# Seven block products of a SwiGLU FFN on one core: another order, three PSUM banks instead of four, and transposes placed later

## The chip, the cores and the metric

One core of a Trainium2 chip runs the whole program. The metric is device microseconds for one execution. A profiled execution gives a trace beside its time; its span, from the program's first to its last instruction, is a little shorter than its time. The engines are TensorE (PE: matmuls and transposes; PEld: its weight loads), VectorE (DVE), ScalarE (ACT), GpSimd (POOL) and SyncE (SP), whose queue issues most DMAs.

## The reference

Two layers, each made of a SwiGLU FFN at half weight, a token mixer, and another such FFN, with a layer norm after each. There are 256 tokens (two tiles of 128, t = 0 and 1) of width 1024; the FFN's inner width is 2816. So there are four FFNs in all:

```python
def swiglu(x, wg, wu, wd):
    return (jax.nn.silu(x @ wg) * (x @ wu)) @ wd
...
x = layer_norm(ALPHA * x + 0.5 * swiglu(x, ffn_wg[l, 0], ffn_wu[l, 0], ffn_wd[l, 0]), ln_g[l, 0], ln_b[l, 0])
```

Everything is float32.

## The kernel before, in words

**Precision.** A float32 product is done as three matmuls: each operand is split in a high and a low part (`xh`, `xl`; `wh`, `wl`), and high times high, high times low and low times high are summed in PSUM (`mm3`, L263). For weights the split is one ACT copy that rounds (`wh`) and one DVE subtraction (`wl`), on tiles of 128x1024 (`split_tile` L217, `split_half` L223). Weights come by DMA into `raw` tiles, of which there are three; `wh` and `wl` have eight buffers each.

**Units.** A unit is 1 MB of weights (two tiles). `units` holds how each one is loaded and split, in the order of use. Using unit u emits the splits up to u + 4 in the middle of an FFN (`ahead` is 3). The inner width is cut in eleven chunks of 256 (gate and up columns side by side: 512 PSUM columns). `down(c)` is the unit that multiplies chunk c's gated values into the output.

**The FFN.** `glu(t, c, q)` adds half q of the input width to chunk c's 512 columns for token tile t: 12 matmuls. After q = 1 the gate follows: silu on ACT (`sg`), and one DVE operation that multiplies (`hh`). `h_T(t, g)` transposes the gated values of chunk pair g on PE and splits them into `hi` (ACT) and `lo` (DVE); `down(t, c)` reads these. A down costs 24 matmuls for both token tiles.

**Strassen's stage.** For chunks 4 and 5, and again for 8 and 9, `strassen` replaces the 8 block products (two token tiles, two halves of the width, two chunks) by seven, after Winograd. The left operands are sums of blocks of x, made once per FFN by `make_sums` (L312); the right ones are sums of weight blocks, made on DVE by `less` (L141) in the functions f1 to f7 of `seven` (L132) and split by `parts`. The seven are spread among four downs of earlier chunks by `SEVEN` (L41): None is a product, a number a down.

**Order.** In the middle of the FFN (`middle` L511) PE's instructions keep the program's order. The order on ACT, DVE and SP is set ahead of time by a scheduler, which goes by program order, by `high_priority`, and by its own estimate of when operands and buffers are ready; on the chip each queue then runs in that fixed order. Groups of chunks follow `GROUPS` (L39): normal chunks 2 and 3, stage 4/5, normal 6 and 7, stage 8/9, normal 10, then the last downs (`end` L534), which are not pinned.

**PSUM.** Eight banks: four hold the output sums (`acc`), four (`g` and `tr`, for t = 0 and 1) are handed out in the order of a list, `self.free` (L376); who is done with a bank appends it.

The places that the change touches: `SEVEN`, `seven`, `strassen` (L421), `gated` (L473), the place of `h_T` and `make_sums` in `middle`, and the scratch size in `kernel`.

Of the kernel before, what the change touches and what calls it, by code (L numbers as in the profile page):

```python
# [18 lines left out]
F32 = mybir.dt.float32  # L19
# [3 lines left out]
AF = mybir.ActivationFunctionType  # L23
ALU = mybir.AluOpType
# [30 lines left out]
def build(ctx, tc, d):  # L55
    nc = tc.nc
    PE, ACT, DVE, POOL = nc.tensor, nc.scalar, nc.vector, nc.gpsimd

    cst = ctx.enter_context(tc.tile_pool(name="cst", bufs=1))
    wp = ctx.enter_context(tc.tile_pool(name="wp", bufs=1))  # L60
    act = ctx.enter_context(tc.tile_pool(name="act", bufs=1))
    mix = ctx.enter_context(tc.tile_pool(name="mix", bufs=2))
# [61 lines left out]
    units = []  # L124
# [4 lines left out]
    def gate_up(l, f, c, q):  # L129
        return [d["wgu"][l, f, c, 2 * q + h] for h in range(2)]  # L130

    def seven(l, f, c):  # L132

        A, B, C, E = [], [], [], []

        def load(to, src, pool, **kw):
            for a in src:
                to.append(pool.tile([128, 1024], F32, **kw))
                last_dma[0] = nc.sync.dma_start(out=to[-1], in_=a)

        def less(a, b, to):  # L141
            for x, y, z in zip(a, b, to):
                DVE.tensor_sub(out=z, in0=x, in1=y)  # L143

        def parts(ts):
            return [split_tile(x, 1024) for x in ts]

        def f1():
            for h, a in enumerate(gate_up(l, f, c, 0)):
                load(A, [a], mix, name="fa", tag=f"qs{h}", bufs=1)  # L150
            return parts(A)

        def f2():
            load(B, gate_up(l, f, c + 1, 0), wp, name="raw", bufs=3)
            less(B, A, A)
            return parts(A)

        def f3():
            load(C, gate_up(l, f, c + 1, 1), mix, name="fc", tag="pT", bufs=3)
            less(C, B, B)  # L160
            return parts(B)

        def f4():
            less(C, A, A)
            return parts(A)

        def f5():
            load(E, gate_up(l, f, c, 1), wp, name="raw", bufs=3)
            return parts(E)

        def f6():
            return parts(C)

        def f7():
            less(E, A, A)
            return parts(A)
        return f1, f2, f3, f4, f5, f6, f7

    for l in range(L):
        def ffn_units(f):  # L180
            def down(c):
                if c >= 0:
                    halves([d["wd"][l, f, (2 * c + h) * 128:(2 * c + h + 1) * 128, :] for h in range(2)], 1024)
            for kind, *cs in GROUPS:
                if kind == "s":
                    fs = iter(seven(l, f, cs[0]))
                    for x in SEVEN:
                        if x is None:
                            units.append(next(fs))
                        else:  # L190
                            down(cs[0] - 4 + x)
# [178 lines left out]
    class Ffn:  # L370
# [50 lines left out]
        def strassen(self, c):  # L421

            s1, s2, s3, s4 = self.s
            a = [[tuple(p[:, 4 * q:4 * q + 4] for p in XT[t]) for q in range(2)] for t in range(2)]
            tags = iter(("c40", "c41", "at011", "vblk"))
            downs = iter(range(c - 4, c))

            def f32(name):
                return mix.tile([128, 512], F32, name=name, tag=next(tags), bufs=1)

            def down():
                n = next(downs)
                self.down(0, n)
                self.down(1, n)
            (w1, b1), (w5, b5) = self.bank(), self.bank()
            self.product(b1, a[0][0])
            with tc.high_priority():
                c11 = f32("c11")
                ACT.activation(out=c11, in_=b1, func=AF.Copy)
            for t in range(2):  # L440
                self.h_T(t, c // 2 - 1)
            down()
            self.product(b5, s1)
            down()
            w7, b7 = self.bank()
            self.product(b7, s3)
            self.product(b1, s2, False)
            with tc.high_priority():
                u = f32("u")
                ACT.activation(out=u, in_=b1, func=AF.Copy)  # L450
                c22 = f32("c22")
                DVE.tensor_add(out=c22, in0=b5, in1=u)
                DVE.tensor_add(out=c22, in0=b7, in1=c22)
            self.gated(1, c + 1, c22)
            down()
            w2, b2 = self.bank()
            self.product(b2, a[0][1])
            with tc.high_priority():
                DVE.tensor_add(out=c11, in0=b2, in1=c11)
            self.gated(0, c, c11)  # L460
            self.product(b5, s4, False)
            with tc.high_priority():
                c12 = f32("c12")
                DVE.tensor_add(out=c12, in0=b5, in1=u)
            self.gated(0, c + 1, c12)
            down()
            self.product(b7, a[1][1], False)
            with tc.high_priority():
                DVE.tensor_add(out=u, in0=b7, in1=u)
            self.gated(1, c, u)  # L470
            self.free.extend((w1, w2, w5, w7))

        def gated(self, t, c, x):  # L473
            with tc.high_priority():
                ACT.activation(out=x[:, 0:256], in_=x[:, 0:256], func=AF.Silu)
                DVE.scalar_tensor_tensor(out=x[:, 0:256], in0=x[:, 0:256], scalar=0.5, in1=x[:, 256:512], op0=ALU.mult,
                                         op1=ALU.mult)
            self.hh.setdefault((t, c // 2), [None, None])[c % 2] = x

        def h_T(self, t, g):  # L480
            src = self.hh.pop((t, g))
# [27 lines left out]
                    c == 0 and kk == 0, c == NCH - 1 and kk == 1)  # L509

        def middle(self):  # L511
            self.s = make_sums(self.sums)
            ahead[0] = 3
            pinned[0] = True
            for kind, *cs in GROUPS[1:]:
                if kind == "s":
                    self.strassen(cs[0])
                    continue
                for c in cs:
                    for q in range(2):  # L520
                        for t in range(2):
                            self.glu(t, c, q)
                        if c % 2 == 0 and q == 0:
                            for t in range(2):
                                self.h_T(t, c // 2 - 1)
# [495 lines left out]
    for l in range(L):  # L1021
# [3 lines left out]
        out = [wout(m, t) for t in range(2)]  # L1025
# [104 lines left out]
```

## Time and profile before

| | before |
|---|---|
| median of 3 runs | 994.06 us (993.55 to 994.34) |
| profiled execution | 994.04 us |
| its span | 991.9 us |
| mean granted clock of PE | 0.997 |
| PE, DVE, ACT, POOL busy | 98%, 79%, 55%, 4% |
| HBM read | 176.91 MB |

Busy is the share of the span in which the engine has an instruction under way. A matmul of 512 columns is shown with some 0.39 us, but the next one starts before it ends; the distance between starts tells what one costs. In a timeline a bracket at the end of a row gives the idle time of the engine ahead of it, and what ended it.

### The profile page before, as it was taken

The page shows a single profiled execution, that of the slowest core. Times are in us where ns is not written, and L with a number is a line of the kernel's source. Part 1 is how long each engine was busy: PE and PEld are TensorE (multiplying, and loading weights), DVE is VectorE, ACT ScalarE, POOL GpSimd, SP SyncE. Part 2 cuts the span into 40 slices and gives each one's busy share as a digit, 9 for nine tenths or more (in the row PEclk, how much of TensorE's full clock was granted, in tenths as well). Part 3 has the DMA queues.
Part 4 walks back from the last instruction along what each step waited for, and adds up shares of the span by engine and source line. Part 5 has one row for each costly group of instructions (what it writes and reads, how often), then busy time and mean ns, then how long its engine had stood idle before and what let it go on. Part 6 is the DMA issues. An engine that isn't in the chain of part 4 may idle for free.

```text
span 991.9 us, 12822 instructions
## 1 busy us (share of the span) xinstructions
PE 971.4 (98%) x4659; PEld 789.1 (80%) x4659; DVE 784.3 (79%) x1195; ACT 549.0 (55%) x840; POOL 34.8 (4%) x50
## 2 busy tenths in 40 slices
PE   8999999999999999999999999999999999999996
PEld 5888878878778888878888788888787788788885
DVE  6698867897869879688797877868888687788775
ACT  6555455475755655565555654644667355555550
POOL 0000000020002000000000000001000010000000
PEclk9999999999999999999999999999999999999999
DMA  8757657554445727537574572675535365473551
GB/s 293 244 163 252 174 171 245 167 191 154 147 152 157 227 84 273 188 138 275 160 223 148 174 253 83 194 237 161 195 102 160 126 222 158 136 251 127 190 171 43
DMA packets 51871, 178.79 MB, mean 180 GB/s; under 512 B 6624, under 2 KB 7648, under 8 KB 51552
## 3 DMA queue, kind: packets, MB, share of 16 engines
q1 hardware_dynamic: 49968, 171.23, 53.1%
q0 software_dynamic: 1840, 6.75, 2.2%
q8 instruction: 36, 0.59, 0.2%
q14 instruction: 27, 0.22, 0.1%
HBM read 176.91 MB, written 1.05 MB: 179 GB/s over the span
## 4 chain that ended last, share of the span: by engine, by line
PE 30%; DVE 10%; DMA 7%; ACT 2%; issue 2%; DVEq 0%; ACTq 0%; SPq 0%
PE acc L266 5%; PE acc L264 5%; PE acc L265 5%; DMA raw<-in_wgu 5%; DVE wl L232 3%; PE tr L418 3%; PE g L418 2%; DMA raw<-in_wd 2%; PE g L265 1%; DVE fa L143 1%; DVE wl L220 1%; PE g L266 1%; PE g L264 1%; ACT wh L231 1%; PE tr L292 1%
## 5 line engine op out<-in xcount | busy, mean ns | idle before, releaser
L232 DVE TENSOR_TENSOR wl<-raw,wh 128x1024 fp32r<-128x1024 f32 (+2 forms) x257 | 308.3, 1206 | 113.0 <-ACT wh L231 112.3
L231 ACT ACTIVATE wh<-raw 128x1024 fp32r<-128x1024 f32 (+2 forms) x257 | 267.9, 1045 | 223.0 <-DMA raw<-in_wgu 76.0
L264 PE MATMUL acc<-wh,hi 128*128 128x512 f32 x352 | 139.4, 396 | 0.0
L265 PE MATMUL acc<-wl,hi 128*128 128x512 f32 x352 | 138.1, 392 | 0.8 <-DVE wl L232 0.8
L266 PE MATMUL acc<-wh,lo 128*128 128x512 f32 x352 | 138.5, 393 | 0.1
L265 PE MATMUL g<-wl,xh 128*128 128x512 f32 (+1 forms) x320 | 122.9, 384 | 1.7 <-DVE wl L232 1.7
L264 PE MATMUL g<-wh,xh 128*128 128x512 f32 (+1 forms) x320 | 123.7, 387 | 0.0
L266 PE MATMUL g<-wh,xl 128*128 128x512 f32 (+1 forms) x320 | 122.5, 383 | 0.0
L219 ACT ACTIVATE wh<-fa 128x1024 fp32r<-128x1024 f32 x64 | 65.2, 1051 | 45.8 <-DVE fa L143 16.9
L220 DVE TENSOR_TENSOR wl<-fa,wh 128x1024 fp32r<-128x1024 f32 x64 | 76.4, 1219 | 4.6 <-ACT wh L219 4.3
L266 PEld LDWEIGHTS acc<-wh,lo 128*128 128x128 f32 x352 | 66.5, 189 | 15.2 <-DVE lo L270 1.2
L265 PEld LDWEIGHTS acc<-wl,hi 128*128 128x128 f32 x352 | 66.4, 189 | 14.6 <-DVE wl L232 1.1
L264 PEld LDWEIGHTS acc<-wh,hi 128*128 128x128 f32 x352 | 66.5, 189 | 13.9 <-ACT wh L231 0.4
L265 PEld LDWEIGHTS g<-wl,xh 128*128 128x128 f32 x320 | 60.3, 188 | 13.7 <-DVE wl L232 3.1
L264 PEld LDWEIGHTS g<-wh,xh 128*128 128x128 f32 x320 | 60.1, 188 | 11.7 <-issue 0.8
L266 PEld LDWEIGHTS g<-wh,xl 128*128 128x128 f32 x320 | 60.1, 188 | 10.8
L264 PE MATMUL tr<-wh,xh 128*128 128x512 f32 x160 | 63.3, 396 | 0.0
L266 PE MATMUL tr<-wh,xl 128*128 128x512 f32 x160 | 62.4, 390 | 0.0
L265 PE MATMUL tr<-wl,xh 128*128 128x512 f32 x160 | 62.3, 390 | 0.0
L143 DVE TENSOR_TENSOR fa<-raw,fa 128x1024 f32<-128x1024 f32 x32 | 38.6, 1221 | 18.8 <-DMA raw<-in_wgu 18.8
L265 PE MATMUL acc<-wl,xh 128*128 128x512 f32 x128 | 51.3, 401 | 1.2 <-DVE wl L232 1.2
L264 PE MATMUL acc<-wh,xh 128*128 128x512 f32 x128 | 50.7, 398 | 0.4 <-ACT wh L231 0.4
(293 smaller groups left out, 1683.4 us busy)
## 6 DMA issues: line engine op xcount, KB each, us to landing
raw<-in_wgu SPq DMA_DIRECT2D x143, 512.0 KB, 4.2
raw<-in_wd SPq DMA_DIRECT2D x88, 512.0 KB, 4.1
raw<-in_win SPq DMA_DIRECT2D x32, 512.0 KB, 3.9
fa<-in_wgu SPq DMA_DIRECT2D x16, 512.0 KB, 4.3
fc<-in_wgu SPq DMA_DIRECT2D x16, 512.0 KB, 4.7
raw<-in_wout SPq DMA_DIRECT2D x16, 512.0 KB, 4.4
lnp_ln_g<-in_ln_g POOLq DMA_DIRECT2D x5, 512.0 KB, 5.4
lnp_ln_b<-in_ln_b POOLq DMA_DIRECT2D x5, 512.0 KB, 5.8
```

The source lines that it names most:

```text
L143: DVE.tensor_sub(out=z, in0=x, in1=y)
L219: ACT.activation(out=wh[:, :w], in_=raw[:, :w], func=AF.Copy)
L220: DVE.tensor_sub(out=wl[:, :w], in0=raw[:, :w], in1=wh[:, :w].bitcast(F32))
L231: ACT.activation(out=wh[:, s], in_=raw[:, s], func=AF.Copy)
L232: DVE.tensor_sub(out=wl[:, s], in0=raw[:, s], in1=wh[:, s].bitcast(F32))
L264: pe(PE.matmul(ps, xh, wh, start=start, stop=False))
L265: pe(PE.matmul(ps, xh, wl, start=False, stop=False))
L266: pe(PE.matmul(ps, xl, wh, start=False, stop=stop))
L292: last_pe[0] = PE.transpose(p[:, i * 128:(i + 1) * 128], s, ident)
L418: pe(PE.matmul(ps, a[:, k, :], w[:, s], start=first and k == 0 and n == 0, stop=k == 3 and n == 2, skip_group_check=True))
```

## The change

- In the stage of seven products bank b1 sums products 1, 6, 7 and 4, with copies of its state by ACT after 1, 6 and 7; b5 sums 5 and 3; b2 holds 2. Before, b1 summed two, b5 two, a fourth bank b7 two, and b2 held one. Three DVE adds are left of five, three ACT copies instead of two. Product 4's gate reads its bank directly.
- The order of products and downs is 1 5 d 6 d 7 d 2 3 d 4; before it was 1 d 5 d 7 6 d 2 3 d 4 in the same names.
- The second weight block (`b12`) gets buffers of its own, `fb0` and `fb1`, instead of two of the three `raw`. The scratch for software DMAs is set to 8192.
- `h_T` of the previous chunk pair comes after product 5 instead of 1 in the stage, and in normal groups after t = 0's second half instead of after both first halves.
- `make_sums` comes after chunk 2 instead of ahead of it.

```diff
-SEVEN = (None, 0, None, 1, None, None, 2, None, None, 3, None)
+SEVEN = "1 5 d 6 d 7 d 2 3 d 4".split()
...
+        def f5():
+            load(b12, gate_up(l, f, c + 1, 0), wp, "fb", ("fb0", "fb1"), 1)
+            less(b12, b11, b11)
+            return parts(b11)
+
+        def f6():
+            load(b22, gate_up(l, f, c + 1, 1), mix, "fc", ("pT", "pT"), 3)
+            less(b22, b11, b11)
+            return parts(b11)
+
+        def f7():
+            less(b22, b12, b12)
+            return parts(b12)
 
         def f2():
-            load(B, gate_up(l, f, c + 1, 0), wp, name="raw", bufs=3)
-            less(B, A, A)
-            return parts(A)
...
+            load(b21, gate_up(l, f, c, 1), wp, "raw", ("raw", "raw"), 3)
+            r = parts(b21)
+            less(b21, b11, b11)
+            return r
...
+        return {"1": f1, "5": f5, "6": f6, "7": f7, "2": f2, "3": lambda: parts(b22), "4": lambda: parts(b11)}
...
+            left = {"1": a[0][0], "5": s1, "6": s2, "7": s3, "2": a[0][1], "3": s4, "4": a[1][1]}
...
+            def copy(b):
+
+                r = f32()
+                ACT.activation(out=r, in_=b, func=AF.Copy)
+                return r
+
             (w1, b1), (w5, b5) = self.bank(), self.bank()
...
+            for x in SEVEN:
+                if x == "d":
+                    self.down(0, n)
+                    self.down(1, n)
+                    n += 1
+                    continue
+                if x == "2":
+                    w2, b2 = self.bank()
+                self.product({"5": b5, "3": b5, "2": b2 if x == "2" else None}.get(x, b1), left[x], x in "152")
+                with tc.high_priority():
+                    if x == "1":
+                        c11 = copy(b1)
+                    elif x == "6":
+                        u = copy(b1)
+                    elif x == "7":
+                        c22 = copy(b1)
+                        DVE.tensor_add(out=c22, in0=b5, in1=c22)
+                        self.gated(1, c + 1, c22)
+                    elif x == "2":
+                        DVE.tensor_add(out=c11, in0=b2, in1=c11)
+                        self.gated(0, c, c11)
+                        self.free.append(w2)
+                    elif x == "3":
+                        DVE.tensor_add(out=u, in0=b5, in1=u)
+                        self.gated(0, c + 1, u)
+                        self.free.append(w5)
+                    elif x == "4":
+                        self.gated(1, c, b1, f32())
+                        self.free.append(w1)
+                if x == "5":
+                    for t in range(2):
+                        self.h_T(t, c // 2 - 1)
...
         def middle(self):
-            self.s = make_sums(self.sums)
...
                     for q in range(2):
                         for t in range(2):
                             self.glu(t, c, q)
-                        if c % 2 == 0 and q == 0:
-                            for t in range(2):
-                                self.h_T(t, c // 2 - 1)
+                            if c % 2 == 0 and (q, t) == (1, 0):
+                                self.h_T(0, c // 2 - 1)
+                                self.h_T(1, c // 2 - 1)
+                    if c == 2:
+                        self.s = make_sums(self.sums)
...
-    nc = bacc.Bacc("TRN2", target_bir_lowering=False, num_devices=1)
+    nc = bacc.Bacc("TRN2", target_bir_lowering=False, num_devices=1, dynamic_dma_scratch_size=8192)
```

## Rows read from the trace of the kernel before

**Rows 1.** The page, part 1: busy time, share of the span, instructions.

```profile
PE 971.4 (98%) x4659; PEld 789.1 (80%) x4659; DVE 784.3 (79%) x1195; ACT 549.0 (55%) x840; POOL 34.8 (4%) x50
```

**Rows 2.** Busy time by stretch: length, each engine (count), clock, DMA share, GB/s.

```profile
542.80:588.50 45.70, 43.84 (x190) 35.73 (x189) 38.12 (x39) 26.79 (x31) 0.00 (x0) 0.96 0.59 196
...
611.10:653.20 42.10, 42.10 (x190) 34.64 (x189) 32.76 (x35) 24.16 (x28) 0.53 (x1) 1.00 0.58 197
```

**Rows 3.** Timeline of PE around 547: start, us, line, operation, [idle before].

```profile
545.49 0.60 PE L487 MATMUL g<-ident,hh 128*128 128x128 f32 x4
547.95 0.66 PE L487 MATMUL g<-ident,hh 128*128 128x128 f32 x4 [1.86 <-DVE hh L404]
```

**Rows 4.** Busy time by stretch, just behind those transposes.

```profile
548.60:552.00 3.40, 3.40 (x10) 2.63 (x9) 1.76 (x4) 1.82 (x3) 0.00 (x0) 0.50 0.39 151
```

**Rows 5.** List of waits: waiter, releaser: us in total, times, longest us.

```profile
PE g L487 <- DVE hh L404: 4.6, 4, 1.9
```

**Rows 6.** Timeline of DVE at the same place.

```profile
545.21 1.22 DVE L143 TENSOR_TENSOR fa<-fc,fa 128x1024 f32<-128x1024 f32 x1
546.35 1.22 DVE L232 TENSOR_TENSOR wl<-raw,wh 128x1024 fp32r<-128x1024 f32 x1
547.48 0.41 DVE L404 SCALAR_TENSOR_TENSOR hh<-sg,g 128x256 f32<-128x256 f32 x1
```

**Rows 7.** Timelines of SP, ACT and PE from 120 to 136.

```profile
120.92 16.10 SPq L228 DMA_DIRECT2D raw<-in_wd  x4
...
133.21 1.06 ACT L231 ACTIVATE wh<-raw 128x1024 fp32r<-128x1024 f32 x1 [4.49 <-DMA raw<-in_wd]
...
133.92 0.39 PE L266 MATMUL acc<-wh,lo 128*128 128x512 f32 x1
...
135.58 0.50 PE L265 MATMUL acc<-wl,hi 128*128 128x512 f32 x1 [0.76 <-DVE wl L232]
```

**Rows 8.** Timelines of PE and DVE around chunk 2's gate, third FFN.

```profile
528.94 0.39 PE L266 MATMUL tr<-wh,xl 128*128 128x512 f32 x1
...
533.38 1.22 DVE L143 TENSOR_TENSOR fa<-raw,fa 128x1024 f32<-128x1024 f32 x1 [2.37 <-DMA raw<-in_wgu]
534.52 0.41 DVE L404 SCALAR_TENSOR_TENSOR hh<-sg,tr 128x256 f32<-128x256 f32 x1
```

**Rows 9.** Timelines of PE, ACT and DVE around chunk 10, third FFN.

```profile
658.62 0.60 PE L487 MATMUL g<-ident,c 128*128 128x128 f32 x4
659.06 0.38 PE L487 MATMUL tr<-ident,u 128*128 128x128 f32 x2
...
659.41 0.48 PE L264 MATMUL tr<-wh,xh 128*128 128x512 f32 x1
...
659.96 0.39 PE L266 MATMUL tr<-wh,xl 128*128 128x512 f32 x1
...
662.23 0.39 PE L264 MATMUL g<-wh,xh 128*128 128x512 f32 x1
...
665.63 0.50 PE L266 MATMUL acc<-wh,lo 128*128 128x512 f32 x1
...
662.66 1.06 ACT L231 ACTIVATE wh<-raw 128x1024 fp32r<-128x1024 f32 x1 [1.81 <-DMA raw<-in_wd]
663.62 0.58 ACT L269 ACTIVATE hi<-g 128x512 fp32r<-128x512 f32 x1
...
664.89 0.68 DVE L270 TENSOR_TENSOR lo<-g,hi 128x512 fp32r<-128x512 f32 x1
```

**Rows 10.** Busy time by stretch in the first FFN, columns as in rows 2.

```profile
12.00:34.00 22.00, 20.36 (x87) 16.13 (x88) 16.19 (x20) 12.15 (x18) 0.00 (x0) 1.00 0.87 300
34.00:56.10 22.10, 22.10 (x103) 18.36 (x102) 17.51 (x18) 13.02 (x17) 0.00 (x0) 1.00 0.71 225
```

**Rows 11.** Groups of instructions: line, operation, shapes, count | busy us, mean ns.

```profile
L459 DVE TENSOR_TENSOR c<-g,c 128x512 f32<-128x512 f32 x8 | 5.5, 683 | 0.0
L439 ACT ACTIVATE c<-tr 128x512 f32<-128x512 f32 x8 | 4.8, 598 | 14.8 <-PE tr L418 14.8
```

More of the change, by code (lines that the diff above doesn't have):

```diff
@@ L132, in seven, with load @@
     def seven(l, f, c):
[L134 to L138, printed above, removed]
+        b11, b12, b21, b22 = [], [], [], []
+        def load(to, src, pool, name, tags, bufs):
+            for a, tag in zip(src, tags):
+                to.append(pool.tile([128, 1024], F32, name=name, tag=tag, bufs=bufs))
                 last_dma[0] = nc.sync.dma_start(out=to[-1], in_=a)
@@ L148, in f1 @@
         def f1():
-            for h, a in enumerate(gate_up(l, f, c, 0)):
-                load(A, [a], mix, name="fa", tag=f"qs{h}", bufs=1)
-            return parts(A)
-        def f2():
-            load(B, gate_up(l, f, c + 1, 0), wp, name="raw", bufs=3)
-            less(B, A, A)
[L156 to L177, printed above, removed]
+            load(b11, gate_up(l, f, c, 0), mix, "fa", ("qs0", "qs1"), 1)
+            return parts(b11)
[6 more added lines that the diff above has]
+            less(b22, b11, b11)
+            return parts(b11)
+        def f7():
+            less(b22, b12, b12)
+            return parts(b12)
+        def f2():
+            load(b21, gate_up(l, f, c, 1), wp, "raw", ("raw", "raw"), 3)
[3 more added lines that the diff above has]
+        return {"1": f1, "5": f5, "6": f6, "7": f7, "2": f2, "3": lambda: parts(b22), "4": lambda: parts(b11)}
     for l in range(L):
@@ L185, in ffn_units @@
                 if kind == "s":
-                    fs = iter(seven(l, f, cs[0]))
+                    fs = seven(l, f, cs[0])
+                    n = cs[0] - 4
                     for x in SEVEN:
-                        if x is None:
-                            units.append(next(fs))
+                        if x == "d":
+                            down(n)
+                            n += 1
                         else:
-                            down(cs[0] - 4 + x)
+                            units.append(fs[x])
                 else:
@@ L424, in strassen @@
             a = [[tuple(p[:, 4 * q:4 * q + 4] for p in XT[t]) for q in range(2)] for t in range(2)]
+            left = {"1": a[0][0], "5": s1, "6": s2, "7": s3, "2": a[0][1], "3": s4, "4": a[1][1]}
             tags = iter(("c40", "c41", "at011", "vblk"))
[L426 to L434, printed above, removed]
@@ L435, in strassen @@
-            (w1, b1), (w5, b5) = self.bank(), self.bank()
[L436 to L439, printed above, removed]
-            for t in range(2):
-                self.h_T(t, c // 2 - 1)
[L442 to L478, printed above, removed]
+            def f32():
+                return mix.tile([128, 512], F32, name="cc", tag=next(tags), bufs=1)
@@ new lines, in copy @@
+            def copy(b):
+                r = f32()
+                ACT.activation(out=r, in_=b, func=AF.Copy)
+                return r
+            (w1, b1), (w5, b5) = self.bank(), self.bank()
+            n = c - 4
+            for x in SEVEN:
+                if x == "d":
+                    self.down(0, n)
+                    self.down(1, n)
+                    n += 1
+                    continue
[25 more added lines that the diff above has]
+                        self.h_T(t, c // 2 - 1)
@@ L480, in h_T, with gated @@
+        def gated(self, t, c, x, to=None):
+            if to is None:
+                to = x
+            ACT.activation(out=to[:, 0:256], in_=x[:, 0:256], func=AF.Silu)
+            DVE.scalar_tensor_tensor(out=to[:, 0:256], in0=to[:, 0:256], scalar=0.5, in1=x[:, 256:512], op0=ALU.mult,
+                                     op1=ALU.mult)
+            self.hh.setdefault((t, c // 2), [None, None])[c % 2] = to
         def h_T(self, t, g):
@@ L517, in middle @@
                     self.strassen(cs[0])
-                    continue
-                for c in cs:
+                for c in (cs if kind == "n" else ()):
                     for q in range(2):
@@ L522, in middle @@
                             self.glu(t, c, q)
-                        if c % 2 == 0 and q == 0:
-                            for t in range(2):
-                                self.h_T(t, c // 2 - 1)
+                            if c % 2 == 0 and (q, t) == (1, 0):
[3 more added lines that the diff above has]
+                        self.s = make_sums(self.sums)
                 if not m0 and cs[0] == 6:
```

## The prediction

> **What bounds the kernel now.** I read the page's busy shares first. TensorE (PE) is busy 98% of the span [rows 1]; that alone proves little, as a pipelined matmul counts as busy while it overlaps the next. So I went to the timeline of PE and took start-to-start distances: in an undisturbed run one 128x512 matmul starts 0.227 us after the other (ten of them from 659.96 to 662.23 [rows 9]). The change has no matmul and no transpose more or less, so the only thing it can win on PE is idle time. Third, the busy times by stretch: each of the eight stages of seven products (first product to last) takes 42.1 us where nothing is late, and 45.7 in the worst of them [rows 2]. VectorE (DVE) is busy 33 of the 42.1 us there, so it is near the bound in this stage but not it. Last, the list of waits and the timeline around the stretches that are longer say what PE waited for.
>
> **The change part by part.**
>
> *The gate wait in front of the transposes (goes).* Before, `h_T` of the previous chunk pair stands right behind the first product. Its second half begins at 547.95, 2.46 us after the first [rows 3]; where nothing waits the distance is 0.44 (658.62 to 659.06; the pair is over at 659.41 by the next matmul, so about 0.79 for both [rows 9]). Lost: 2.02, of which the list of waits shows 1.9 as idle, since the last transposes still drain. It has four such waits with 4.6 us idle in all [rows 5]; at 0.16 more each, from start to start (2.02 less the 1.86 that the row of 547.95 has in brackets), they cost 5.2. The cause is DVE's queue: a subtraction and a split of weights, which are not yet wanted, stand ahead of the gate `hh` [rows 6]. After the change product "5" stands between, 12 x 0.227 = 2.7 us more. The gate of 547.48 ended at 547.89 and its transposes would be wanted at 545.49 + 2.7 + 0.4 = 548.6: late by nothing, with 0.7 to spare. What would be late next is the down, and it reads the older `h`.
>
> *The clock behind it (goes).* After the 2.0 us wait the granted clock is 0.50 from 548.6 to 552.0, that is 1.2 instead of 2.4 GHz [rows 4]: half of 3.4 us, 1.7 lost. Behind the other three the clock stayed up.
>
> *The second half of a down's weights (goes).* `f2` keeps its block B12 in two of the three `raw` buffers, so the downs load through the one that is left: four loads take 16.1 us to issue, ACT waits 4.49 us for one of them, and PE stands at 135.58 [rows 7]. From the matmul of 133.92 to the second behind it, 135.58, it is 1.66 instead of 0.45. Now B12 has buffers of its own: 1.2 goes.
>
> Sum of what goes: 5.2 + 1.7 + 1.2 = 8.1 us.
>
> *Fewer adds, one copy more.* Per such stage DVE loses two adds of 0.683 and ACT gains one copy of 0.598 [rows 11]: over eight, DVE -10.9, ACT +4.8. I cost it at nothing: both engines have their weights ready ahead of PE there, and where that cover is gone it is at most a queue delay of one copy. The copies between two products on one bank could hold PE, but each time a down (24 x 0.227 = 5.4 us) lies between the copy and the next product on it, against 0.6 for the copy. Product 4 writes the bank two products and a down after its last copy. The subtractions are eight before and after.
>
> *make_sums one chunk later.* Seven DVE operations of about 0.68 move behind the chunk's splits: 4.8 us, by the add of that shape [rows 11]. "5" wants its first sum 2.7 us behind the first product, a chunk behind the place where it is made. Nothing, as DVE has 4.6 us idle in the first FFN's pair of chunks (17.51 of 22.10 busy [rows 10]) and weights wait ready; without that cover at most 4.8 a FFN.
>
> *Transposes later in the normal groups (adds).* `h_T` moves behind t = 0's second half. Two things become tight. (a) Banks: the list of free banks is served in order, and t = 0's bank comes back before `h_T` takes two, so the next chunk's first product writes just that bank, 0.8 + 2.7 = 3.5 us after it was filled; before, it took one that had been free for long. The bank is free when silu and gate have read it. In the third FFN that took from 529.2 (the matmul of 528.94 and its 0.23) to 534.9 [rows 8]: 5.8 us, 2.2 too long. But there the gate stood behind a subtraction that waited 2.37 us for B12's load through `raw` [rows 8], and behind two splits of `h_T` (2 x 0.6) that now come later; without both it is done in time. Bounds 0 and 4 x 2.2 = 8.9; I take 1.0, for the first FFN, whose ACT queue waits for transfers. (b) Chunk 10: the down follows `h_T` after one product instead of two. Its `lo` ended at 665.57, 6.95 us behind the first transpose of 658.62, and PE already waited for it (665.63 [rows 9]). After the change its third matmul stands 0.8 + 2.7 + 0.5 = 4.0 us behind, so 2.9 would be missing if the distance held. I expect it not to hold: ACT gets to `hi` only behind the splits that wait for their transfers (idle 1.81 before 662.66, `hi` at 663.62 [rows 9]), and these end at the same place of PE's work whenever the transposes were. No later split can slip ahead, since it needs buffers that PE frees after the last chunk. Only silu and gate of t = 0 can now come first (0.4 on DVE). Bounds 0 and 4 x 2.9 = 11.6; I take 2.0: 0.5 in two FFNs and 1.0 in the first.
>
> The Trainium skill (PSUM — Partial Sum Buffer, "Engine vs sequencer instructions") says that ScalarE and VectorE work through their queues in strict order. The trace agrees: ACT stood idle 1.81 us for a transfer while `hi` behind it had had its transposes since 659. By that rule (a) and (b) have a price at all; if `hi` and the gate could overtake, both would be nothing and the sum 3.0 lower.
>
> *B12's buffers are free from the start (adds).* SP can issue their two loads of 512 KB early in the first FFN, where 300 GB/s are moved and the DMA engines are 87% busy [rows 10]: 1.75 us each. The next 22 us have room (71%). Bounds 0 and 3.5; I take 0.5, since two other early loads already sit in the gaps and would move back.
>
> *Half the scratch for software DMAs.* POOL is busy 4% [rows 1]; its transfers are parameters for a norm far ahead. Nothing.
>
> *The even spread of the downs* changes which unit stands before which, with the same eleven per stage. Nothing beyond the above.
>
> Sum: -8.1 + 1.0 + 2.0 + 0.5 = -4.6. The profiled execution took 994.04 (span 991.9), the median of the runs shown is 994.06, so no step between them: **989.4 us**.
>
> **The rivals.**
>
> *No change: what goes in one wait comes back in others.* The terms (a), (b) and the early loads at half of their bounds, 4.4 + 5.8 + 1.75, outweigh 8.1; at a third, 2.9 + 3.9 + 1.2 = 8.0, they cancel it: 994. For it: DVE's and ACT's orders are fixed ahead, and every late gate in this trace comes from operations placed ahead of it. Against: the idle time for B12's load, which stood ahead of the gates, goes.
>
> *Slower: the gate and `lo` keep their distance from PE.* Place: the chunk after each `h_T`, and the down of chunk 8. Price 8.9 + 11.6 - 8.1 = 12.4: 1006; with one fall of the clock more, 1008. It decides as soon as the eight places lose over 1.0 us each on average. For it: 5.8 and 6.95 us as shown. Against: the reasons under (a) and (b). A milder form, half of it with the early loads, is 998.
>
> *Everything goes and nothing comes:* 994.0 - 8.1 = 986. For it: (a) is zero wherever the gate comes within 3.5 us.
>
> *The waits at `h_T` stay,* because DVE's queue gets more subtractions before the gate and it slips by 2.7: then only 1.2 goes and 3.5 comes, 996.
>
> **How the numbers follow.** Forecast (988 to 992) 0.46; everything goes (985.5 to 988) 0.15; no change, with the waits that stay, 0.23; slower 0.16. A difference under 0.2% (2 us) can't be told from none here. The forecast's own range is 986 to 992. Leaving out a twentieth below and a tenth above gives 985.5 to 997. Faster by over 0.2% (under 992.07) takes the first two cases: 0.61; within 0.2%, 0.22; slower, 0.17.
>
> **What would show it.** Right: no idle of PE before the second transposes of such a stage, no 0.50 clock inside the third FFN, 42 us in all eight stages, DVE some 11 us less busy. Wrong: PE waiting on a bank at the first product of chunks 3 or 7 (released by the gate, L404 before), PE waiting for `hi` or `lo` at the down of chunk 8 for over 1 us in each FFN, or idle of PE between 25 and 40 us for transferred weights. A loss in the mixing stage, which the change doesn't touch, would be wrong in a way that none of these cases has.

## The result, and the profile after

The changed kernel took 987.43 us (median of six runs, 986.09 to 988.62), the kernel before 993.62 beside it (six runs, 990.58 to 994.34): a ratio of 0.9940, 95% interval 0.9925 to 0.9956. The gain is 6.2 us, where 4.6 were forecast. The profiled execution took 986.09, with a span of 984.3 against 991.9.

The page of the changed kernel (busy us, share of the span, instructions) shows PE as busy as before, in a shorter span [rows 1]:

```profile
PE 969.4 (98%) x4659; PEld 789.4 (80%) x4659; DVE 779.4 (79%) x1179; ACT 561.4 (57%) x848; POOL 34.5 (4%) x50
```

DVE has the 16 instructions less and ACT the 8 more that the diff gives. The busy times moved by other amounts than the forecast's -10.9 and +4.8, by -4.9 and +12.4. Neighbours that overlap are counted once in them, and fewer splits now stand back to back: added up one by one (count times mean, over all groups), DVE's instructions fell by 11.5 us and ACT's rose by 6.1.

The busy time by stretch of the third FFN's two stages of seven products (length, then PE, PEld, DVE, ACT, POOL, granted clock, DMA share, GB/s) answers to [rows 2 and 4]; the two rows behind are the first FFN's start, for [rows 10]:

```profile
540.36:582.41 42.05, 42.05 (x190) 34.62 (x188) 33.03 (x33) 26.12 (x30) 0.00 (x0) 1.00 0.69 224
605.06:647.11 42.05, 42.05 (x190) 34.62 (x189) 31.72 (x32) 24.95 (x29) 0.53 (x1) 1.00 0.59 206
12.00:34.00 22.00, 20.52 (x89) 16.03 (x88) 15.98 (x21) 12.93 (x18) 0.00 (x0) 1.00 0.83 301
34.00:56.10 22.10, 22.10 (x103) 18.40 (x102) 17.29 (x19) 12.95 (x17) 0.00 (x0) 1.00 0.70 240
```

All eight stages now take 42.05 us from the first product to the last. Before they took 42.05, 43.52, 42.76, 42.80, 45.71, 42.05, 43.94 and 42.05, so they gave back 8.5. The first product of all starts 1.0 later (57.11 instead of 56.12). The span is 7.6 shorter, so the rest of it is as long as before to 0.1 us.

The place of the worst wait, the transposes of the third FFN's first stage, in the timelines of PE and DVE [rows 3 and 6]:

```profile
545.88 0.60 PE L485 MATMUL tr<-ident,hh 128*128 128x128 f32 x4
546.32 0.60 PE L485 MATMUL g<-ident,hh 128*128 128x128 f32 x4
546.67 0.48 PE L262 MATMUL acc<-wh,hi 128*128 128x512 f32 x1
...
541.43 0.41 DVE L402 SCALAR_TENSOR_TENSOR hh<-sg,g 128x256 f32<-128x256 f32 x1
```

The second half follows 0.44 us behind the first, as in the undisturbed case. But look at when the gate ran: its last half begins at 541.43, before even product 5 started (543.09). It is in time not for the 2.7 us that it was given, but because it came earlier: 1.07 us behind the stage's first product (540.36), where before it began 4.7 us behind it (547.48 against 542.76).

The whole list of PE's waits of the changed kernel (us in total, times, longest) has no row for the gate any more [rows 5]; most of what is left lies in the start:

```profile
PE acc L290 <- DMA x<-in_x: 1.8, 1, 1.8
PE acc L263 <- DVE wl L230: 1.6, 3, 1.0
PE acc L104 <- DVE zw L107: 1.2, 1, 1.2
PE g L263 <- DVE wl L230: 0.8, 2, 0.4
PE tr L290 <- ACT c L652: 0.6, 2, 0.3
PE acc L262 <- ACT wh L229: 0.5, 1, 0.5
PE tr L290 <- DMA x<-in_x: 0.3, 1, 0.3
```

SP's timeline at the down of [rows 7]: three loads into `raw` take 6.66 us to issue, where four took 16.10, and B12 goes into `fb` beside them.

```profile
119.71 6.66 SPq L226 DMA_DIRECT2D raw<-in_wd  x3
127.57 0.33 SPq L140 DMA_DIRECT2D raw<-in_wgu  x1
128.71 1.55 SPq L140 DMA_DIRECT2D fb<-in_wgu  x2
```

The two places that the forecast feared, in the timelines of PE and DVE. First (a), chunk 2's first bank in the third FFN [rows 8]; then (b), the down behind chunk 10 [rows 9]:

```profile
525.63 0.39 PE L264 MATMUL tr<-wh,xl 128*128 128x512 f32 x1
...
529.48 0.39 PE L262 MATMUL tr<-wh,xh 128*128 128x512 f32 x1
...
527.73 0.41 DVE L402 SCALAR_TENSOR_TENSOR hh<-sg,tr 128x256 f32<-128x256 f32 x1
...
655.27 0.60 PE L485 MATMUL tr<-ident,cc 128*128 128x128 f32 x4
...
658.88 0.39 PE L262 MATMUL acc<-wh,hi 128*128 128x512 f32 x1
659.33 0.39 PE L264 MATMUL acc<-wh,lo 128*128 128x512 f32 x1
...
658.27 0.68 DVE L268 TENSOR_TENSOR lo<-tr,hi 128x512 fp32r<-128x512 f32 x1
```

(a): the bank is full at 525.86 (525.63 and 0.23), the gate ends at 528.14, so it is held 2.3 us, and the product that takes it again starts at 529.48. Before, the hold was 5.8. (b): `lo` is there at 658.95, 3.7 us behind the first transpose (before: 6.95), and the down's third matmul, which wants it, starts without idle time.

### The profile page after: what moved, and what is told of

It reads as the page before. It is cut to its first block, busy times and chain, and to the rows that moved or that the text cites. A ratio compares the mean times of both kernels' runs of the same rounds, so it can differ in the third digit from the quotient of the medians.

```text
span 984.3 us, 12817 instructions
## 1 busy us (share of the span) xinstructions
PE 969.4 (98%) x4659; PEld 789.4 (80%) x4659; DVE 779.4 (79%) x1179; ACT 561.4 (57%) x848; POOL 34.5 (4%) x50
## 4 chain that ended last, share of the span: by engine, by line
PE 47%; DVE 2%; issue 1%; ACT 1%; DVEq 0%
PE acc L262 6%; PE acc L264 6%; PE acc L263 6%; PE g L416 5%; PE g L263 3%; PE g L264 3%; PE g L262 3%; PE tr L416 3%; PE tr L262 2%; PE tr L264 2%; PE tr L263 2%; PE tr L290 1%; PE acc L281 1%; DVE wl L230 1%; PE g L485 1%
## 5 line engine op out<-in xcount | busy, mean ns | idle before, releaser
L263 PE MATMUL g<-wl,xh 128*128 128x512 f32 (+1 forms) x288 | 110.8, 385 | 0.8 <-DVE wl L230 0.8
L262 PE MATMUL g<-wh,xh 128*128 128x512 f32 (+1 forms) x288 | 110.7, 385 | 0.0
L264 PE MATMUL g<-wh,xl 128*128 128x512 f32 (+1 forms) x288 | 110.7, 384 | 0.0
L262 PE MATMUL tr<-wh,xh 128*128 128x512 f32 x192 | 75.4, 393 | 0.0
L264 PE MATMUL tr<-wh,xl 128*128 128x512 f32 x192 | 74.8, 389 | 0.0
L263 PE MATMUL tr<-wl,xh 128*128 128x512 f32 x192 | 74.8, 389 | 0.0
L263 PEld LDWEIGHTS g<-wl,xh 128*128 128x128 f32 x288 | 54.1, 188 | 12.3 <-DVE wl L230 2.3
L262 PEld LDWEIGHTS g<-wh,xh 128*128 128x128 f32 x288 | 54.1, 188 | 11.4 <-ACT wh L229 0.8
L264 PEld LDWEIGHTS g<-wh,xl 128*128 128x128 f32 x288 | 54.2, 188 | 9.4
L264 PE MATMUL acc<-wh,xl 128*128 128x512 f32 x128 | 51.3, 401 | 0.1
```

What stands on the lines that cost most here:

```text
L262: pe(PE.matmul(ps, xh, wh, start=start, stop=False))
L263: pe(PE.matmul(ps, xh, wl, start=False, stop=False))
L264: pe(PE.matmul(ps, xl, wh, start=False, stop=stop))
```

## What had to be settled

The gates come early now. The prediction has one reason (product 5 stands between, call it PLACE) and the diff holds another, which it counted only for a down's weights: B12 no longer takes two of the three `raw` buffers (BUFFERS). These buffers are given out in turn, and each load waits for the next one; below they are called the ring. ACT's waits for transferred weights point to the second. The rows are those of the kernel before and then of the changed kernel (ACT's split of a weight, waiting for a transfer: us in total, times, longest):

```profile
ACT wh L231 <- DMA raw<-in_wgu: 76.0, 60, 3.5
ACT wh L231 <- DMA raw<-in_wd: 70.5, 50, 4.5
```

```profile
ACT wh L229 <- DMA raw<-in_wgu: 56.7, 53, 3.2
ACT wh L229 <- DMA raw<-in_wd: 29.7, 22, 4.0
```

146.5 us fell to 86.4. Below, "ACT's waits" is the sum of these two rows. Each ratio is to the kernel before, run on the same chip in the same series. The median of the kernel before went from 993.62 to 997.51 between series, so times of different series compare only roughly.

## Experiments: place or buffers

**The changed kernel, transposes back behind product 1.** Only the place is undone.

```
-                if x == "5":
+                if x == "1":
                     for t in range(2):
                         self.h_T(t, c // 2 - 1)
```

> The kernel after, with the transposes of the stage put back behind product 1; B12 keeps its own buffers. Theory PLACE (the prediction's): the 2.7 us of product 5 took the gate waits away, so most of 5.2 + 1.7 us comes back: 991 to 994 us, PE idle for the gate at three or four of the eight stages. Theory BUFFERS: the gate is on time because DVE no longer waits for B12's load in front of it; in the trace after, the gate of t = 1 of chunk 3 or 7 ends 1.5 to 1.9 us behind its product in seven stages and 3.7 in the first, and the transposes would want it at 3.2: only the first stage waits, 0.5 us, so 987 to 988.5 us.

Measured: 987.21 us (984.26 to 989.41), ratio 0.9912 (0.9894 to 0.9931): as fast as with the place changed (987.43 in the series of the result). Of four gate waits one is left in its list of PE's waits:

```profile
PE g L485 <- DVE hh L402: 0.7, 1, 0.7
```

It stands in the first FFN, at 59.94; that stage takes 42.90 us, the other seven 42.01. PLACE is worth 0.85 us in one stage of eight, not 5.2 and a fall of the clock.

**The kernel before, its transposes moved behind product 5.** Only the place is done. In this kernel a down lies ahead of product 5, so they come 8.2 us later, not 2.7.

```
             self.product(b1, a[0][0])
...
-            for t in range(2):
-                self.h_T(t, c // 2 - 1)
             down()
             self.product(b5, s1)
+            for t in range(2):
+                self.h_T(t, c // 2 - 1)
```

> The kernel before, with the stage's transposes moved behind product 5 (which there comes a down later, so 8.2 us later than before); B12 stays in raw. Both theories: the gate waits and the fall of the clock go (gates end at most 5.3 us behind their products), the down's wait of 1.2 us stays: 986.5 to 988 us. If the waits only move on, to the down that reads the transposes' result: 990 to 994.

Measured: 993.9 us (990.12 to 998.95, twelve runs), ratio 0.9992 (0.9973 to 1.0011): nothing. The 986.5 to 988 that both theories gave is missed; the time is the one given for waits that only move on, though they moved to other transposes and not to the down. Seven stages do come down to 42.0 to 42.3, so the wait is gone from where it was; one stage still takes 43.57. The stages give back some 7 us, and later places take them. The rows of the largest, from PE's timeline and the busy time by stretch, are the next transposes of the third FFN, at chunk 10, whose gate is the last one of a stage of seven:

```profile
660.27 0.44 PE L487 MATMUL tr<-ident,u 128*128 128x128 f32 x2 [2.20 <-DVE u L476]
...
661.35:664.76 3.41, 3.41 (x10) 2.63 (x9) 2.22 (x2) 1.38 (x3) 0.00 (x0) 0.50 0.81 244
```

PE waits 2.2 us and then works 3.4 us at a granted clock of 0.50, which costs 1.7 more. The transposes at chunk 6 in that FFN wait 1.1 us for the same kind of gate; the remaining 2 us are spread over the rest. ACT's waits here are 154.9 (79.8 and 75.1): the shortage is untouched, and PE pays for it at later places.

**The kernel before with B12's own buffers.** Only the buffers are done (and the smaller scratch that makes room for them).

```
-            load(B, gate_up(l, f, c + 1, 0), wp, name="raw", bufs=3)
+            for h, a in enumerate(gate_up(l, f, c + 1, 0)):
+                load(B, [a], wp, name="fb", tag=f"fb{h}", bufs=1)
```

> The kernel before, with two buffers of its own for B12 and the scratch of 8192; all else as before. PLACE: only the wait of the down goes, -1.2: 992 to 993 us, with the four gate waits still there. BUFFERS: the gates come on time too and nearly all of the gain is there: 986 to 989 us, all eight stages near 42.05 us.

Measured: 986.5 us (984.84 to 989.3), ratio 0.9912 (0.9896 to 0.9929): all of the gain. The stages take 42.05 (42.23 the first), with the old order, banks, adds and transposes. ACT's waits are 86.4, the changed kernel's number.

**The changed kernel with B12 back in the ring.** (The scratch is the larger one of before again.)

```
-            load(b12, gate_up(l, f, c + 1, 0), wp, "fb", ("fb0", "fb1"), 1)
+            load(b12, gate_up(l, f, c + 1, 0), wp, "raw", ("raw", "raw"), 3)
```

> The kernel after, with B12 in two of the three raw buffers again and the default scratch; order, banks and transposes as after. If B12's buffers are worth just the wait of the second down (1.2 us): 988 to 989.5 us. If they are also what keeps the gates on time, the gates fall back to 3 to 5.8 us behind their products and the reused bank (wanted after 3.5 us) holds up PE at chunk 3 or 7: 0.6 + 0.8 + 0.8 + 2.2 + 1.9 = 6.3 us more, 993 to 996 us, with PE idle at the first product of chunk 3.

Measured: 1030.29 us (1027.61 to 1031.82), ratio 1.0346 (1.0326 to 1.0365). Neither theory had this: without the buffers the rest of the change costs some 35 us over the kernel before. Its waits, PE's first and then ACT's:

```profile
PE acc L262 <- ACT hi L267: 12.3, 4, 4.0
PE g L262 <- DVE hh L402: 5.8, 4, 2.9
PE acc L262 <- ACT wh L229: 4.8, 4, 2.0
...
ACT wh L229 <- DMA raw<-in_wd: 130.8, 64, 7.8
ACT wh L229 <- DMA raw<-in_wgu: 90.0, 69, 5.6
```

The first two rows are (b) and (a): the down behind chunk 10 waits for `hi`, and the first product of a chunk waits for a gate to free its bank. The timelines of ACT, DVE and PE in the third FFN show how a late transfer becomes a late bank:

```profile
618.73 1.06 ACT L229 ACTIVATE wh<-raw 128x1024 fp32r<-128x1024 f32 x1 [1.75 <-DMA raw<-in_wgu]
619.70 1.99 ACT L217 ACTIVATE wh<-fa 128x1024 fp32r<-128x1024 f32 x2
621.59 0.36 ACT L401 ACTIVATE sg<-g 128x256 f32<-128x256 f32 x1
...
619.83 1.23 DVE L230 TENSOR_TENSOR wl<-raw,wh 128x1024 fp32r<-128x1024 f32 x1 [1.59 <-ACT wh L229]
620.97 2.35 DVE L218 TENSOR_TENSOR wl<-fa,wh 128x1024 fp32r<-128x1024 f32 x2
623.24 0.42 DVE L402 SCALAR_TENSOR_TENSOR hh<-sg,g 128x256 f32<-128x256 f32 x1
...
616.80 0.39 PE L264 MATMUL g<-wh,xl 128*128 128x512 f32 x1
623.71 0.50 PE L262 MATMUL g<-wh,xh 128*128 128x512 f32 x1 [2.91 <-DVE hh L402]
```

The bank is full at 617.03 (616.80 and 0.23). ACT waits 1.75 us for a weight, DVE 1.59 for ACT, the gate stands behind both and two more splits, and PE gets its bank when the gate ends at 623.66. The clock adds to it: five stretches, 30.7 us together, ran at a granted clock of 0.50 (1.2 instead of 2.4 GHz). PE was busy for 26.5 us of them, so some 13 are lost. Three of the five by stretch, and behind them the stretch around the wait just shown, where the clock stayed up:

```profile
144.50:154.73 10.23, 7.78 (x18) 5.18 (x18) 3.50 (x3) 2.95 (x3) 0.00 (x0) 0.50 0.48 156
499.48:506.30 6.82, 6.22 (x16) 4.86 (x17) 4.25 (x6) 2.23 (x4) 0.00 (x0) 0.50 0.76 244
694.04:697.45 3.41, 3.19 (x7) 2.09 (x8) 3.41 (x7) 1.91 (x4) 0.00 (x0) 0.50 0.45 133
...
614.00:626.00 12.00, 9.09 (x45) 7.29 (x44) 9.10 (x12) 7.42 (x10) 0.00 (x0) 1.00 0.68 210
```

## Experiments: what about the buffers

Two more buffers can help because the ring stays deep while B12 is held (DEPTH), because B12's loads need not stand in the ring's order (OWN SLOT), or because any more weights in flight help, or the smaller scratch.

**The kernel before with a ring of five**, run in two series:

```
-            load(B, gate_up(l, f, c + 1, 0), wp, name="raw", bufs=3)
+            load(B, gate_up(l, f, c + 1, 0), wp, name="raw", bufs=5)
```

(and so at the two other allocations of `raw`). The scratch is the smaller one, here and in the ring of four.

> Theory DEPTH (the ring of three raw buffers starves the weight splits while B12 holds two of them; with two more buffers the ring keeps three for the others): with a ring of five and B12 still in it the gate waits and the late half of a down's weights go as with B12's own buffers, 985 to 988 us, and all eight stages take 42.05. Rival OWN SLOT (what counts is that B12's two loads have a place of their own and can be issued long before, out of the ring's turn): the loads of B12 still stand in the ring's order behind the other weights, the gates stay late, 991 to 994.

> The kernel before with a ring of five, beside the changed kernel with the same ring. It took 983.9; the same again, 983 to 986. If this second series lies over 986, the lead over the changed kernel (987.4) isn't settled.

Measured: 983.93 us (ratio 0.9895, 0.9873 to 0.9917) and 984.57 (0.9871, 0.9847 to 0.9895). DEPTH holds and OWN SLOT falls; 983.93 is a little under DEPTH's 985 to 988, and the second series lies in the 983 to 986 that it was given. All stages take 42.05, and ACT's waits are down to 6.6.

**The kernel before, the two buffers given to B21** (the other block that goes through `raw`, `E` in this kernel). B12 stays in the ring of three; the scratch is the smaller one.

```
-            load(E, gate_up(l, f, c, 1), wp, name="raw", bufs=3)
+            for h, a in enumerate(gate_up(l, f, c, 1)):
+                load(E, [a], wp, name="fb", tag=f"fb{h}", bufs=1)
```

> The two buffers of 4 KB and the halved scratch are spent on the block B21 instead, and B12 stays in the ring of three. DEPTH and HOLD (two of three buffers are kept by B12 from its load until its last split): nothing of it goes in front of the second products, 992 to 994, with the waits at the transposes behind the first product as before. Rival (any 8 KB more of weights in flight, or the halved scratch, does it): 985 to 988.

Measured: 991.66 us (989.48 to 995.89), ratio 0.9966 (0.9948 to 0.9985): a third of the gain of the ring of five, a little more than DEPTH expected. Three gate waits stay, and ACT's waits are 139.4. So the smaller scratch and just any 8 KB make a third of it at most; which of the two makes that third isn't separated.

```profile
PE g L488 <- DVE hh L405: 2.9, 3, 1.4
```

**The kernel before with a ring of four**, the smallest dose.

> The kernel before with a ring of four, B12 in it. Under DEPTH the downs' weights then have two buffers instead of one while B12 holds two: ACT's waits for transferred weights of gate and up and of down, 146 us together with a ring of three, fall to between 50 and 90, most of the gate waits go, 985 to 989. If a fixed shortage is behind the waits (the DMA's rate), four change little: 991 to 994.

Measured: 984.89 us (984.56 to 985.26), ratio 0.9874 (0.9845 to 0.9903). One buffer of 4 KB per partition does all of it, better than expected; ACT's waits are 24.2 (the second row of this kind is 3.7):

```profile
ACT wh L231 <- DMA raw<-in_wgu: 20.5, 20, 3.0
```

The traces show how the ring made the gates late. The rows are from the timelines of SP and DVE in the third FFN, first of the kernel before, then with the ring of four:

```profile
527.57 9.99 SPq L139 DMA_DIRECT2D raw<-in_wgu  x2
540.33 1.23 DVE L143 TENSOR_TENSOR fa<-raw,fa 128x1024 f32<-128x1024 f32 x1 [1.66 <-DMA raw<-in_wgu]
...
520.45 3.06 SPq L139 DMA_DIRECT2D raw<-in_wgu  x2
540.27 0.41 DVE L404 SCALAR_TENSOR_TENSOR hh<-sg,g 128x256 f32<-128x256 f32 x1
```

With three buffers the two loads of B12 take 9.99 us to issue. DVE itself waits 1.66 us for the second of them, subtracts, and from there works without a gap up to the late gate of 547.48. Such a wait of DVE (1.66 to 1.85 us) stands ahead of all four late gates; it stands ahead of three more stages too, where the gate was in time all the same. With four buffers the loads take 3.06 us to issue and that wait is gone. The gate of 540.27 then begins 1.08 us behind the stage's first product (539.19), instead of 4.7. It still has a subtraction and a split of weights just ahead of it, as before [rows 6]: the order right ahead of the gate is the same, and DVE gets there earlier.

**The changed kernel with a ring of five**, B12 in it: is the rest of the change worth anything once weights are not short?

> The changed kernel with B12 in the ring and a ring of five, the same memory as now. If the ring's depth is all that the change's gain rests on, it goes as the kernel before does with a ring of five: 983 to 986, and product order, copies, spread and the later transposes are worth under 2 us together. If the changed order needs B12 apart from the ring (it holds B12 over two downs, the old order over one): 990 to 1000. If the new order is worth something of its own on top of the ring: under 981.

Measured: 985.46 us (984.88 to 985.93), ratio 0.9880 (0.9855 to 0.9904), beside 984.57 (984.12 to 984.93) for the kernel before with the same ring in the same series. ACT's waits are 5.1. That is the first of the three cases. Order, spread, copies for adds and later transposes together are worth nothing that helps; they may cost 0.9 us, which is below what was set as tellable.

The dose in one table (time: median; waits: ACT's, in us):

| kernel | ring, and what holds two of it | waits | time |
|---|---|---|---|
| before | 3, B12 and B21 | 146.5 | 993.6 to 997.5 by series |
| before, B21 own | 3, B12 | 139.4 | 991.66 |
| before, B12 own | 3, B21 | 86.4 | 986.50 |
| changed | 3, B21 | 86.4 | 987.43 |
| before | 4, B12 and B21 | 24.2 | 984.89 |
| before | 5, B12 and B21 | 6.6 | 983.93 |
| changed | 5, B12 and B21 | 5.1 | 985.46 |
| changed | 3, B12 (over two downs) and B21 | 220.8 | 1030.29 |

## Experiments: the prices of the rest of the change

**B12 in the ring, transposes of the normal groups at their old place.** The kernel of 1030 us with one more edit undone:

```
-                            if c % 2 == 0 and (q, t) == (1, 0):
-                                self.h_T(0, c // 2 - 1)
-                                self.h_T(1, c // 2 - 1)
+                        if c % 2 == 0 and q == 0:
+                            for t in range(2):
+                                self.h_T(t, c // 2 - 1)
```

> The changed kernel with B12 in the ring of three (1030 us) and, besides, the normal groups' transposes at their old place, behind both halves of the first product. If the later place of those transposes is what makes late weights dear (the bank that the next chunk's product waits for, 5.8 us in four waits; the waits for hi and lo at the down of chunk 8, 14 us in eight; the clock behind them), then most of that goes: 1010 to 1016. If the late weights cost PE the same wherever the transposes stand: 1026 to 1032.

Measured: 1014.45 us (1013.46 to 1015.61), ratio 1.0198 (1.0172 to 1.0224): some 15 us come from the later place alone, and the time is in the range expected. ACT's waits are as long as before this edit (225.6), so the shortage is the same; what changed is how much of it reaches PE. So the later place, which the prediction's terms (a) and (b) are about, does have a price when gates are late.

**The same, with B12 held over one down instead of two.**

```
-SEVEN = "1 5 d 6 d 7 d 2 3 d 4".split()
+SEVEN = "1 d 5 d 6 7 d 2 3 d 4".split()
```

> The changed kernel with B12 in the ring of three, the normal groups' transposes at their old place (1014.5 us, ACT's waits for transferred weights 226 us), and the downs in the order that holds B12 over one down instead of two. That order by itself costs some 8.5 us (a wait for the copy of 0.86 to 1.9 in each of eight stages). If the time that B12 holds two of three buffers is what the changed order adds: the waits fall to 150 to 190 us and the time, with those 8.5 in it, is 1000 to 1010. If the hold makes no difference: waits of 215 or more and 1020 to 1025.

Measured: 1009.96 us (1009.64 to 1016.09), ratio 1.0166 (1.0121 to 1.0210), at the upper end of the range for the hold. ACT's waits are 144.6, a little under it and the length that they have in the kernel before. PE waits for no gate any more, but for the copy of a bank:

```profile
PE tr L416 <- ACT cc L432: 9.3, 4, 2.9
PE g L416 <- ACT cc L432: 6.4, 4, 2.3
```

So the order of the downs is what makes the changed kernel starve the ring of three. That it does so by the hold is the reading that was expected; the edit also moves two downs among the other loads, and no run separates the two. What is left of the time is the other effect of this edit, products 6 and 7 side by side on one bank: 15.7 us of waits, more than the 8.5 expected for it, since here the copies are late too.

**The changed kernel with that order, and B12's own buffers.** The price of a copy between two products with no down to hide it:

```
-SEVEN = "1 5 d 6 d 7 d 2 3 d 4".split()
+SEVEN = "1 d 5 d 6 7 d 2 3 d 4".split()
```

> The changed kernel with the downs in another order, so that products 6 and 7 on the same bank follow one another with no down between: product 7 has to wait for the copy of the bank. By the prediction's step (a copy of 0.6 us costs nothing only because a down of 5.4 us lies between): each of eight stages loses 0.6 to 1.5 us, 992 to 999 us, and the stages take 42.7 to 43.5. Rival (the wait is hidden, or swallowed by PE's queue): 987 to 988, stages of 42.05.

Measured: 996.92 us (995.13 to 1000.28), ratio 1.0014 (0.9995 to 1.0032), as the prediction's step had it. It is 9.5 over the changed kernel of another series; by the two ratios it is 7.4, and by the stages 8.8. Seven of them take 43.01 (0.96 more each), the first 44.08. PE's timeline around one of the eight waits:

```profile
380.24 0.40 PE L416 MATMUL g<-wh,sb 128*128 128x512 f32 x1
381.33 0.50 PE L416 MATMUL g<-wh,sa 128*128 128x512 f32 x1 [0.69 <-ACT cc L432]
```

1.09 us from start to start instead of 0.23. The prediction's condition for costing the copies at nothing was the right one: a down between.

## Why the prediction came out as it did

**What goes was sized rightly, its main reason was wrong.** 8.1 us was to go from the eight stages, and 8.5 went. But 6.9 of the 8.1 was put to a step that fails: *"After the change product '5' stands between, 12 x 0.227 = 2.7 us more."* With the transposes behind product 1 again the gates are still in time (987.21), and with nothing but the transposes moved the waits only change their place and the time stays (ratio 0.9992). What the runs show in its place: the ring of `raw` buffers was one short. B12 held two of three while downs and the next products pulled their weights through the third, and its own second half came late through the same ring. ACT and DVE waited for transfers, DVE in the end 1.66 us for B12 itself (540.33), and the gate, in order behind the work that had been held up, came late. The prediction saw this ring, at the down of [rows 7], and priced it at 1.2 us, the one wait that the split weights caused directly; under (a) it saw DVE's wait for B12's load ahead of another gate [rows 8]. It also named the queue ahead of the gate rightly as the cause [rows 6]. What it missed is that the two are one thing: the queue was late because the ring was.

**Why the wrong reason gave nearly the right sum.** The wait was priced by what PE loses there, and that is the same whichever part of the change takes it away. So the nearness of 8.1 to 8.5 is luck as far as the reason goes. A wrong part would have shown only in a kernel that has one and not the other. The signs that were to show the forecast right couldn't show it either: PE without idle time before the transposes and 42 us in all eight stages come with either cause.

**The terms that were to come.** 3.5 was forecast, and nothing of it is seen. (a) was taken at 1.0: it is 0, the worst first bank of the eight is held 3.3 us against 3.5 to spare (3.29, the first FFN's chunk 2). (b) was taken at 2.0: no stall of PE over 0.12 us stands at any of the four downs. The reason given, that the splits ahead of `hi` end *"at the same place of PE's work whenever the transposes were"*, fits the third FFN (`lo` at 658.95 for a matmul at 659.33; before, 665.57 for 665.63 [rows 9]) and the first; in the second and fourth `lo` comes some 2 us before it is wanted, as the transfers are earlier. The early loads of B12 were taken at 0.5: PE's busy time in the first FFN's two stretches is 20.52 and 22.10, against 20.36 and 22.10 [rows 10], so they cost nothing there. What did come is 1.0 us in the first 12 us, where PE waits 1.8 us for the input `x`. The start of the first product moved between 55.15 and 57.11 over the kernels run here, and the kernel before with the place alone changed, which has no early load, is at 56.99; so this is not put to the change.

**Costed at nothing, and nothing:** fewer adds, `make_sums` a chunk later and the spread. The chunk pairs take 22.65 us in all four FFNs, before and after, and with a ring of five in both kernels all of the rest together makes 0.1%. The copies cost nothing too; between the last of them and product 4 lie two downs, where the prediction counted one.

**The rivals.** The outcome lies in one of them: 987.43 is in the 985.5 to 988 of *everything goes and nothing comes*, which was given 0.15, and not in the 988 to 992 of the forecast's own case (0.46). Its condition, the gate within 3.5 us, is met everywhere. The slower one, *the gate and `lo` keep their distance from PE*, is in kind the kernel with B12 in the ring: the same two places, and falls of the clock. That kernel is 24 us dearer than its 1006, with 13 us of its loss in the first FFN's two stages (46.0 and 51.2 us), where the weights of downs come late. Its point of decision was misnamed, though. It is decided by the ring of weights, ahead of ACT and DVE. The argument against it, that the idle time for B12's load goes, was sound: that is the wait of DVE at 540.33.

**The order of the queues.** In the kernel with B12 in the ring of three the bank is full at 617.03, yet the silu of 621.59 and the gate of 623.24 come behind splits that waited for a transfer. The late gate of the kernel before is of the same kind: its silu was over at 544.21, and it began at 547.48, behind a subtraction and a split [rows 6]. The Trainium skill (PSUM — Partial Sum Buffer, "Engine vs sequencer instructions") says that the queues of ScalarE and VectorE keep a strict order. Both traces agree.

## What to carry to other kernels

When a wait shows an engine's queue as late, follow that queue back to the first thing in it that waited for a transfer before pricing a move of the waiting instruction: a move takes the wait away at one place and leaves the lateness for the next. A big block that borrows buffers of a small shared ring is to be counted as the ring's depth less what it holds, for as long as it holds it; one more buffer of 4 KB per partition was worth here all that the reordered kernel gained, and more (984.9 against 987.4 us, medians of two series; ratios 0.9874 and 0.9940). Do one part of a change alone before believing in the part that the argument liked.

## What was not expected of the hardware

ACT's waits for transferred weights fell from 146.5 us to 24.2 with one more buffer, though the same bytes move, so the rate of the DMA was not what was short. The time also varied less from run to run: 990.98 to 1001.66 us in 23 runs of the kernel before, 983.62 to 985.32 in six with the ring of five beside them. PE lost far less than ACT waited: 146.5 us of such waits cost the kernel before some 10 us, and 220.8 cost the changed order 45 (1030.29 less the 985.46 with a ring of five). Part of that is the clock: in the changed kernel with B12 in the ring of three, idle times of PE of 3.8 and 4.0 us behind chunk 10 (second and third FFN) go with a granted clock of 0.50 for 6.8 and 3.4 us, while the 2.9 us at 623.71 left it at 1.00. The length of the idle time alone doesn't tell: 1.86 us in the kernel before was followed by 3.4 us at 0.50 [rows 3 and 4].
